# Four experts of a float32 mixture: column tiles of one width put one after another over four feature blocks

## The chip, the core and the metric

The kernel runs on one core of a Trainium2 chip. The metric is the device time of one execution in microseconds (us), as the median of several runs. One further execution is recorded by the hardware profiler; all rows shown below are from that one.

## The reference

A trunk of two layers over 256 positions of width 1024, all in float32. What matters here is the last sub-layer, a mixture of eight experts of which each position takes two:

```
logits = h @ w_router
top_v, top_i = lax.top_k(logits, TOP_K)          # TOP_K = 2 of N_EXPERTS = 8
gates = jax.nn.softmax(top_v, axis=-1)
...
for e in range(N_EXPERTS):
    y = y + dense_gate[..., e:e + 1] * swiglu(h, w_gate[e], w_up[e], w_down[e])

def swiglu(h, w_gate, w_up, w_down):
    return (jax.nn.silu(h @ w_gate) * (h @ w_up)) @ w_down
```

An expert's gate and up matrices are 1024 x 3584, its down matrix 3584 x 1024.

## The kernel before, in words

The experts are sorted by how many positions chose them; the rank in that order decides how many places an expert gets. Rank 0 has 128 places. Ranks 1 to 3 (`SMALL`) have 64 (`PLACES`). Ranks 4 to 7 (`MIDDLE`) have 64 and 32 more (`MORE`), 96 in all. They run in the order `RANKS`: 0, 1, 7, 6, 2, 5, 4, 3. Positions beyond the places go through a branch at the end (`overflow`).

**Weights.** An expert's weights come in 84 halves of 512 KB (128 x 1024 float32); eight experts have 672. `Stream` loads them in a fixed order into the pool `wp` of 30 tiles (`NW`), all through SP's queue (line 159). Each load takes the tile that was loaded 30 loads earlier and waits until the last reader of that tile is done; eight loads are on the way at most. When the program is written, `Stream` counts the tiles in use (`live`) and writes loads ahead while `live` is below `NW - ROOM`. `ROOM` is 4 in all of the expert part.

**Steps.** An expert of ranks 1 to 7 has 3584 hidden features in seven groups of 512. They are done in four steps: three long ones of two groups side by side, and a short one of the last group, split into two of 256 columns. A step computes gate (`pg`) and up (`pu`), then the product `act`, then `act` is transposed (`psT`). One step later comes its share of the output (`y`). For the short step that share is done by `down_half`, one output half at a time, and it falls behind the first `both` or `up_gate` of the next expert.

**Tiles of TensorE.** 64 places fill half the columns of the 128 x 128 array, so two such matmuls, with other weights, run side by side (`halves_of`). For the middle ranks the 32 further places go into four 32-wide column tiles side by side: `pm` holds up and gate of both groups, `ym` the output. `both` goes through the eight 128-row blocks of the 1024 features one by one: for each, gate and up with 64-wide tiles (line 1205), then the four 32-wide ones (line 1207). `down` and `down_half` do the same for `y` (lines 1263 and 1285) and `ym` (line 1233). A float32 matmul stands in the trace as two records, a pass each.

**Small work between.** `st.soon(n, ...)` puts a piece of work off by n beats, and a beat is one half drawn from the stream (`next(ws)`). In this way the gather of the next expert's positions (`psg`, read by ScalarE into `hs`), the transposes (`psT`, `psTm`) and the scatter of the last expert's output (`pssc`, read by VectorE) get their places among the matmuls. Gather, transposes and scatter share two PSUM buffers (`pst`). The engines run their instructions in the order in which the program has them.

Of the kernel before, what the change touches and what calls it, by code (L numbers as in the profile page):

```python
# [23 lines left out]
KD = D // P  # L24
S = 256
# [9 lines left out]
RANKS = (0, 1, 7, 6, 2, 5, 4, 3)  # L35
SMALL = (1, 2, 3)
PLACES = 64
MIDDLE = (4, 5, 6, 7)
MORE = 32
# [14 lines left out]
def trunk_(es, tc, stream, experts, blocks, x, xT, c, columns, ada_w, ln_g, ln_b, ev_w_in, pool_w, ev_sink, ev_w_out,  # L54
          od_w_in, od_sg_ln_g, od_sg_ln_b, w_sT, od_b_s, od_w_out, ffn_w_gate, ffn_w_up, ffn_w_down, out):
    nc = tc.nc
    V, A, G, T = nc.vector, nc.scalar, nc.gpsimd, nc.tensor
# [201 lines left out]
    st = Stream()  # L259
# [189 lines left out]
    with ExitStack() as ph:  # L449
# [50 lines left out]
        for g, w in enumerate(WINDOWS):  # L500
            r = w // 2
# [44 lines left out]
        h = big([P, KD, S], F32, name="h")  # L546
# [153 lines left out]
        for g in range(4):  # L700
            psg.append(bank())
            for t in range(NT):
                T.matmul(psg[g][:, 0:S], lhsT=pt[:, t, g * P:(g + 1) * P], rhs=band[:, g, t, :],
                         start=t == 0, stop=t == NT - 1)
# [5 lines left out]
        for g in range(4):  # L710
            ps = psg[g][:, S:2 * S]
# [4 lines left out]
        ws = []  # L716
# [91 lines left out]
        ws = [list(st.get()) for _ in range(2)]  # L808
# [14 lines left out]
        z, h = norm_modulate(y, gates[0, 2], folded, hf, gu_tile)  # L823
# [77 lines left out]
        ws = list(st.get()) + list(st.get())  # L901
# [6 lines left out]
        z, h = norm_modulate(y, gates[0, 5], (sa, sb), hf, v_half)  # L908
# [15 lines left out]
        for n in range(2):  # L924
            if n:
                ps2 = [psa.tile([P, 512], F32, tag="a", name="psv") for _ in range(NT)]
                for u in range(2):
                    for k, w in enumerate(st.get()):
                        kk = u * 4 + k
# [5 lines left out]
        for t in range(NT):  # L935
            mv = sml.tile([P, 2], F32, tag="mv", name="mv")
            V.bn_aggr(mv, s6s[t])
            mu, rs = rstd_of(mv)
# [4 lines left out]
        for u in range(4):  # L943
            if u == 3:
                st.AHEAD = 4
            ps = psa.tile([P, 2, S], F32, tag="a", name="psu")
# [7 lines left out]
        for g in range(0, 8, 2):  # L954
            ps = psa.tile([P, 2, NT, P], F32, tag="a", name="pssv")
# [114 lines left out]
    with ExitStack() as ph:  # L1070
# [118 lines left out]
        def both(step, h, pg, pu, pm):  # L1189


            s, fs = step
            ws = st.get()
            for kk in range(0, KD, 2):
                w = [next(ws) for _ in range(4 * len(fs))]
                for k in range(2):
                    if len(fs) == 2:
                        g, u = (w[k], w[2 + k]), (w[4 + k], w[6 + k])
                    else:
                        g, u = ((a[:, 0:S], a[:, S:2 * S]) for a in (w[k], w[2 + k]))  # L1200
                    n = g[0].shape[-1]
                    flags = dict(start=kk + k == 0, stop=kk + k == KD - 1)
                    for ps, pair in ((pg, g), (pu, u)):
                        for rows_, a in zip(halves_of, pair):
                            T.matmul(ps[rows_, 0:n], lhsT=h[:, kk + k, 0:PLACES], rhs=a, **flags)  # L1205
                    for b, a in enumerate(u + g):
                        T.matmul(pm[b * MORE:(b + 1) * MORE, 0:n], lhsT=h[:, kk + k, PLACES:], rhs=a, **flags)  # L1207
            for _ in ws:
                pass

# [40 lines left out]
        def down(step, aT, y):  # L1251
            s, fs = step
            small = RANKS[s] in SMALL + MIDDLE
            if fs[-1] == NFE - 1:
                for n in range(2):
                    down_half(step, aT, y, n)
            elif small:
                ws = st.get()
                for kk in range(4):
                    pair = [next(ws) for _ in range(2)]  # L1260
                    for n in range(2):
                        for rows_, w in zip(halves_of, pair):
                            T.matmul(y[n][rows_, :], lhsT=aT[0][:, kk, rows_], rhs=w[:, n * 512:(n + 1) * 512],  # L1263
                                     start=fs[0] == 0 and kk == 0, stop=False)
                    if RANKS[s] in MIDDLE:
                        for b, w in enumerate(pair):
                            down_more(aT[1], kk, b, [(n, w[:, n * 512:(n + 1) * 512]) for n in range(2)], y[2],
                                      fs[0] == 0 and kk == 0, False)
                for _ in ws:
                    pass  # L1270
            else:
                for u in range(2):
                    for k, w in enumerate(st.get()):
                        kk = u * 2 + k
                        for n in range(2):
                            mm3(y[n], sl2(aT, lambda a: a[:, kk, :]), sl2(w, lambda a: a[:, n * 512:(n + 1) * 512]),
                                fs[0] == 0 and kk == 0, False)

        def down_half(step, aT, y, n):

            ws = list(st.get())
            if RANKS[step[0]] in SMALL + MIDDLE:
                for k in range(2):
                    for b, rows_ in enumerate(halves_of):
                        T.matmul(y[n][rows_, :], lhsT=aT[0][:, k, rows_], rhs=ws[b * 2 + k], start=False, stop=k == 1)  # L1285
                    if RANKS[step[0]] in MIDDLE:
                        for b in range(2):
                            down_more(aT[1], k, b, [(n, ws[b * 2 + k])], y[2], False, k == 1)
            else:
                for k, w in enumerate(ws):  # L1290
                    mm3(y[n], sl2(aT, lambda a: a[:, k, :]), w, False, k == 3)
# [159 lines left out]
        for i, step in enumerate(steps):  # L1451
# [17 lines left out]
            if (s, fs[0]) == (1, 2):  # L1469
                for t in range(NT):  # L1470
                    A.activation(xt[t], xt[t], AF.Copy, scale=ALPHA)
            if (s, fs[0]) == (3, 0):
                lng, lnb = affine_rows(1, 1)
            h, ohT = cur
# [150 lines left out]
```

## Time and profile before

| | |
|---|---|
| median of 3 runs | 1353.6 us (1352.05 to 1355.18) |
| profiled execution | 1348.47 us, span 1346.7 us |
| TensorE matmul (PE) busy | 1315.8 us, 98% of the span |
| VectorE (DVE) busy | 522.9 us, 39% |
| ScalarE (ACT) busy | 323.1 us, 24% |
| DMA | 470.49 MB, mean 349 GB/s |
| granted TensorE clock, mean | 0.996 of full speed |

Busy is the time in which at least one instruction of the engine was running. Matmuls are pipelined and their ends are modelled, so starts say more of TensorE than durations do. The rank 7 expert starts at 619 us, rank 2 at 886.9, rank 5 at 976.1 and rank 3 at 1241 us; the last matmul of the experts ends about 1334 us.

### The profile page before, as it was taken

The page shows a single profiled execution, that of the slowest core. Times are in us where ns is not written, and L with a number is a line of the kernel's source. Part 1 is how long each engine was busy: PE and PEld are TensorE (multiplying, and loading weights), DVE is VectorE, ACT ScalarE, POOL GpSimd, SP SyncE. Part 2 cuts the span into 40 slices and gives each one's busy share as a digit, 9 for nine tenths or more (in the row PEclk, how much of TensorE's full clock was granted, in tenths as well). Part 3 has the DMA queues.
Part 4 walks back from the last instruction along what each step waited for, and adds up shares of the span by engine and source line. Part 5 has one row for each costly group of instructions (what it writes and reads, how often), then busy time and mean ns, then how long its engine had stood idle before and what let it go on. Part 6 is the DMA issues. An engine that isn't in the chain of part 4 may idle for free. (4 is left out here: it accounts for less than half of the span.)

```text
span 1346.7 us, 19701 instructions
## 1 busy us (share of the span) xinstructions
PE 1315.8 (98%) x7360; PEld 675.1 (50%) x7360; DVE 522.9 (39%) x812; ACT 323.1 (24%) x504; POOL 16.5 (1%) x82
## 2 busy tenths in 40 slices
PE   6999999999998999999999999999999999999997
PEld 4758999987866887442323233324423222323332
DVE  7697999947856986300200020012011001100102
ACT  0416444426227774310110011001001001100100
POOL 1000000000000000000000000000000000000001
PEclk9999999999989999999999999999999999999999
DMA  9997889991874799999999988999999998889993
GB/s 376 409 409 278 330 328 360 363 365 69 333 297 156 277 341 358 409 409 409 409 409 409 409 347 303 375 365 409 409 409 409 409 377 316 307 322 371 404 409 123
DMA packets 129576, 470.49 MB, mean 349 GB/s; under 512 B 14520, under 2 KB 14656, under 8 KB 129472
## 3 DMA queue, kind: packets, MB, share of 16 engines
q1 hardware_dynamic: 129168, 468.89, 90.0%
q8 instruction: 59, 0.97, 0.3%
q14 instruction: 45, 0.37, 0.1%
q10 hardware_dynamic: 304, 0.27, 0.1%
HBM read 468.05 MB, written 1.05 MB: 348 GB/s over the span
## 5 line engine op out<-in xcount | busy, mean ns | idle before, releaser
L196 DVE TENSOR_TENSOR lo<-raw,hi 128x1024 fp32r<-128x1024 f32 x158 | 186.4, 1220 | 32.1 <-ACT hi L195 25.6
L195 ACT ACTIVATE hi<-raw 128x1024 fp32r<-128x1024 f32 x158 | 159.0, 1053 | 67.0 <-PE y L371 12.8
L1263 PE MATMUL y<-raw,ah 128*64 128x512 f32 x672 | 160.4, 602 | 0.3 <-DMA raw<-in_experts 0.2
L1493 DVE TENSOR_TENSOR act<-act,pu 128x512 f32<-128x512 f32 (+1 forms) x16 | 9.9, 621 | 317.4 <-PE pu L1205 317.4
L1205 PE MATMUL pg<-raw,hs 128*64 128x512 f32 (+1 forms) x512 | 125.5, 564 | 0.2 <-DMA raw<-in_experts 0.2
L1207 PE MATMUL pm<-raw,hs 128*32 128x512 f32 (+1 forms) x1024 | 122.7, 551 | 0.0
L271 DVE CUSTOM_DVE_ANT_0 raw<-raw,cond,colt 128x1024 f32<-128x1024 f32 x96 | 118.7, 1281 | 8.2 <-DMA raw<-in_stream 8.2
L1205 PE MATMUL pu<-raw,hs 128*64 128x512 f32 (+1 forms) x512 | 119.0, 539 | 0.4 <-DMA raw<-in_experts 0.3
L1488 ACT ACTIVATE act<-pg 128x512 f32<-128x512 f32 (+1 forms) x35 | 19.4, 554 | 345.7 <-PE pg L1205 258.2
L369 PE MATMUL psgu<-hh,hi 128*128 128x256 f32 x320 | 91.2, 285 | 0.0
L371 PE MATMUL psgu<-hh,lo 128*128 128x256 f32 x320 | 90.6, 283 | 0.0
L370 PE MATMUL psgu<-hl,hi 128*128 128x256 f32 x320 | 89.9, 281 | 0.0
L1263 PEld LDWEIGHTS y<-raw,ah 128*64 128x64 f32 x672 | 43.5, 136 | 91.1 <-issue 76.2
L1185 PE MATMUL pu<-raw,hs 128*64 128x512 f32 (+1 forms) x384 | 76.6, 542 | 0.0
L1185 PE MATMUL pg<-raw,hs 128*64 128x512 f32 (+1 forms) x384 | 75.4, 541 | 0.0
L1498 DVE TENSOR_TENSOR act<-act,pu 128x512 f32<-128x512 f32 (+1 forms) x19 | 12.2, 643 | 147.3 <-PE pu L1185 147.3
L1205 PEld LDWEIGHTS pg<-raw,hs 128*64 128x64 f32 x512 | 25.6, 134 | 84.9 <-issue 76.5
L1233 PE MATMUL ym<-raw,am 128*32 128x512 f32 x448 | 68.0, 605 | 0.0
L1205 PEld LDWEIGHTS pu<-raw,hs 128*64 128x64 f32 x512 | 36.9, 137 | 61.1 <-issue 52.8
L1207 PEld LDWEIGHTS pm<-raw,hs 128*32 128x32 f32 x1024 | 20.1, 108 | 90.2 <-issue 87.0
L1333 DVE SCALAR_TENSOR_TENSOR x<-pssc,by_rank,x 128x512 f32<-128x512 f32 x28 | 20.8, 748 | 104.6 <-PE pssc L1331 104.6
L369 PEld LDWEIGHTS psgu<-hh,hi 128*128 128x128 f32 x320 | 60.7, 190 | 0.4
(303 smaller groups left out, 1655.4 us busy)
## 6 DMA issues: line engine op xcount, KB each, us to landing
raw<-in_experts SPq DMA_DIRECT2D x668, 512.0 KB, 10.1
raw<-in_stream SPq DMA_DIRECT2D x204, 512.0 KB, 7.4
lng<-in_ln_g SPq DMA_DIRECT2D x4, 512.0 KB, 7.9
lnb<-in_ln_b SPq DMA_DIRECT2D x4, 512.0 KB, 9.0
xT<-in_xT SPq DMA_DIRECT2D x2, 512.0 KB, 7.7
x<-in_x SPq DMA_DIRECT2D x2, 512.0 KB, 10.2
guest<-in_experts SPq DMA_DIRECT2D x2, 512.0 KB, 10.1
guests<-in_experts SPq DMA_DIRECT2D x2, 512.0 KB, 6.8
```

The costliest lines, as they stand in the source:

```text
L195: A.activation(hi, raw, AF.Copy)
L196: V.tensor_tensor(lo, raw, hi, op=ALU.subtract)
L271: V.tensor_tensor_reduce(raw[:, 0, :], raw[:, 0, :], cond, 1.0, adab[:, i:i + 1], ALU.mult, ALU.add, accum_out=mod[l, part][:, kk:kk + 1])
L369: T.matmul(ps, lhsT=l[0], rhs=r[0], start=start, stop=False)
L370: T.matmul(ps, lhsT=l[0], rhs=r[1], start=False, stop=False)
L371: T.matmul(ps, lhsT=l[1], rhs=r[0], start=False, stop=stop)
L1185: T.matmul(ps[rows_, 0:w.shape[-1]], lhsT=h[:, kk + k, :], rhs=w, start=kk + k == 0, stop=kk + k == KD - 1)
L1205: T.matmul(ps[rows_, 0:n], lhsT=h[:, kk + k, 0:PLACES], rhs=a, **flags)
L1207: T.matmul(pm[b * MORE:(b + 1) * MORE, 0:n], lhsT=h[:, kk + k, PLACES:], rhs=a, **flags)
L1233: T.matmul(y[q * MORE:(q + 1) * MORE, :], lhsT=am[:, k, b * MORE:(b + 1) * MORE], rhs=a, start=first, stop=last)
L1263: T.matmul(y[n][rows_, :], lhsT=aT[0][:, kk, rows_], rhs=w[:, n * 512:(n + 1) * 512], start=fs[0] == 0 and kk == 0, stop=False)
L1333: V.scalar_tensor_tensor(yacc[t][:, sl], ps, gate_by[:, t, r:r + 1], yacc[t][:, sl], op0=ALU.mult, op1=ALU.add)
```

## The change

For the middle ranks the feature blocks are taken four at a time: all gate matmuls of the four, then all up matmuls, then all 32-wide ones. In `down` all four blocks of `y` come ahead of all four of `ym`, and in `down_half` both blocks of `y` ahead of both of `ym`. The halves for a group are drawn from the stream before its matmuls are written. `ROOM` becomes 9 for middle ranks and stays 4 for the others. No matmul, load or other operation is added or left out.

```diff
--- before.py
+++ after.py
@@ -1191,20 +1191,25 @@
 
             s, fs = step
             ws = st.get()
-            for kk in range(0, KD, 2):
-                w = [next(ws) for _ in range(4 * len(fs))]
-                for k in range(2):
-                    if len(fs) == 2:
-                        g, u = (w[k], w[2 + k]), (w[4 + k], w[6 + k])
-                    else:
-                        g, u = ((a[:, 0:S], a[:, S:2 * S]) for a in (w[k], w[2 + k]))
-                    n = g[0].shape[-1]
-                    flags = dict(start=kk + k == 0, stop=kk + k == KD - 1)
-                    for ps, pair in ((pg, g), (pu, u)):
-                        for rows_, a in zip(halves_of, pair):
-                            T.matmul(ps[rows_, 0:n], lhsT=h[:, kk + k, 0:PLACES], rhs=a, **flags)
+
+            for k0 in range(0, KD, 4):
+                rs = []
+                for u in range(2):
+                    w = [next(ws) for _ in range(4 * len(fs))]
+                    for k in range(2):
+                        if len(fs) == 2:
+                            rs.append((k0 + u * 2 + k, (w[k], w[2 + k]), (w[4 + k], w[6 + k])))
+                        else:
+                            rs.append((k0 + u * 2 + k, *((a[:, 0:S], a[:, S:2 * S]) for a in (w[k], w[2 + k]))))
+                n = rs[0][1][0].shape[-1]
+                flags = lambda kk: dict(start=kk == 0, stop=kk == KD - 1)
+                for i, ps in ((1, pg), (2, pu)):
+                    for r in rs:
+                        for rows_, a in zip(halves_of, r[i]):
+                            T.matmul(ps[rows_, 0:n], lhsT=h[:, r[0], 0:PLACES], rhs=a, **flags(r[0]))
+                for kk, g, u in rs:
                     for b, a in enumerate(u + g):
-                        T.matmul(pm[b * MORE:(b + 1) * MORE, 0:n], lhsT=h[:, kk + k, PLACES:], rhs=a, **flags)
+                        T.matmul(pm[b * MORE:(b + 1) * MORE, 0:n], lhsT=h[:, kk, PLACES:], rhs=a, **flags(kk))
             for _ in ws:
                 pass
 
@@ -1256,13 +1261,16 @@
                     down_half(step, aT, y, n)
             elif small:
                 ws = st.get()
+                pairs = []
                 for kk in range(4):
                     pair = [next(ws) for _ in range(2)]
+                    pairs.append(pair)
                     for n in range(2):
                         for rows_, w in zip(halves_of, pair):
                             T.matmul(y[n][rows_, :], lhsT=aT[0][:, kk, rows_], rhs=w[:, n * 512:(n + 1) * 512],
                                      start=fs[0] == 0 and kk == 0, stop=False)
-                    if RANKS[s] in MIDDLE:
+                if RANKS[s] in MIDDLE:
+                    for kk, pair in enumerate(pairs):
                         for b, w in enumerate(pair):
                             down_more(aT[1], kk, b, [(n, w[:, n * 512:(n + 1) * 512]) for n in range(2)], y[2],
                                       fs[0] == 0 and kk == 0, False)
@@ -1283,7 +1291,8 @@
                 for k in range(2):
                     for b, rows_ in enumerate(halves_of):
                         T.matmul(y[n][rows_, :], lhsT=aT[0][:, k, rows_], rhs=ws[b * 2 + k], start=False, stop=k == 1)
-                    if RANKS[step[0]] in MIDDLE:
+                if RANKS[step[0]] in MIDDLE:
+                    for k in range(2):
                         for b in range(2):
                             down_more(aT[1], k, b, [(n, ws[b * 2 + k])], y[2], False, k == 1)
             else:
@@ -1469,6 +1478,8 @@
             if (s, fs[0]) == (1, 2):
                 for t in range(NT):
                     A.activation(xt[t], xt[t], AF.Copy, scale=ALPHA)
+            if fs[0] == 0 and s > 0:
+                st.ROOM = 9 if RANKS[s] in MIDDLE else 4
             if (s, fs[0]) == (3, 0):
                 lng, lnb = affine_rows(1, 1)
             h, ohT = cur
```

The order shows the effect on TensorE at two places. An entry names the line, the tile written, what is read, and the tile's columns by the moving columns; x8 stands for eight such matmuls, and a float32 matmul counts once here. The line numbers behind the change are those of the changed file.

First place: the second step of rank 7 in `both`, where the scatter of rank 1 (`pssc`) and the gather for rank 6 (`psg`) fall. Before:

```order
L1205 MATMUL pg<-raw,hs 64x512 x2
L1205 MATMUL pu<-raw,hs 64x512 x2
L1207 MATMUL pm<-raw,hs 32x512 x4
L1331 MATMUL pssc<-yhl,ohT 128x512 x2
L1088 MATMUL psg<-oh,z 128x96 x8
...
L1331 MATMUL pssc<-yhl,ohT 128x512 x4
```

And with the change:

```order
L1209 MATMUL pg<-raw,hs 64x512 x8
L1209 MATMUL pu<-raw,hs 64x512 x8
L1212 MATMUL pm<-raw,hs 32x512 x16
L1340 MATMUL pssc<-yhl,ohT 128x512 x2
L1088 MATMUL psg<-oh,z 128x96 x8
L1340 MATMUL pssc<-yhl,ohT 128x512 x4
```

The turn of 2, 2 and 4 matmuls, eight to a step, has become one of 8, 8 and 16, two to a step. Between the gather and the two further scatters (x4) there were two turns; now there is nothing.

Second place: `down` of the first step of rank 7, which follows. Before:

```order
L1263 MATMUL y<-raw,ah 64x512 x4
L1233 MATMUL ym<-raw,am 32x512 x4
...
L1219 MATMUL psT<-ident,act 128x128 x4
L1088 MATMUL psg<-oh,z 128x96 x8
L1224 MATMUL psTm<-ident,actm 128x64 x4
```

And with the change:

```order
L1270 MATMUL y<-raw,ah 64x512 x8
L1224 MATMUL psT<-ident,act 128x128 x4
L1088 MATMUL psg<-oh,z 128x96 x8
L1229 MATMUL psTm<-ident,actm 128x64 x4
L1270 MATMUL y<-raw,ah 64x512 x8
L1238 MATMUL ym<-raw,am 32x512 x16
```

The transposes and the second gather stood behind two blocks of `y` and `ym`; now they stand behind two blocks of `y`, in the middle of the 64-wide run. On SP's queue the loads keep their order; only the two row loads `lng` and `lnb` come five places earlier.

## Rows read from the trace of the kernel before

**Rows 1.** The page, its first line.
```profile
span 1346.7 us, 19701 instructions
```

**Rows 2.** Windows of four expert stretches: busy us and instructions by engine, granted clock, DMA.
```profile
619.00:886.90 267.90, 267.24 (x1608) 76.52 (x1606) 26.57 (x50) 22.81 (x49) 0.00 (x0) 1.00 0.97 379
886.90:976.10 89.20, 89.20 (x456) 34.21 (x454) 10.71 (x20) 9.93 (x22) 0.00 (x0) 1.00 1.03 408
976.10:1241.00 264.90, 264.90 (x1608) 76.23 (x1604) 26.97 (x52) 22.82 (x49) 0.00 (x0) 1.00 0.95 365
1241.00:1326.50 85.50, 84.81 (x418) 30.01 (x414) 9.46 (x14) 6.02 (x11) 0.00 (x0) 1.00 0.95 376
```

**Rows 3.** Waits of PE, 619 to 1326.5 us: us in total, times, longest.
```profile
PE pu L1205 <- DMA raw<-in_experts: 0.3, 1, 0.3
```

**Rows 4.** Timeline, rank 2 gate, weight loads alone: start, duration, engine, line.
```profile
888.28 0.14 PEld L1185 LDWEIGHTS pg<-raw,hs 128*64 128x64 f32 x2 [0.28 <-issue]
...
892.57 0.14 PEld L1185 LDWEIGHTS pg<-raw,hs 128*64 128x64 f32 x2 [0.29 <-issue]
```

**Rows 5.** Timeline, rank 7, `both` of a long step, TensorE alone.
```profile
702.90 1.08 PE L1205 MATMUL pg<-raw,hs 128*64 128x512 f32 x4
...
704.77 1.06 PE L1207 MATMUL pm<-raw,hs 128*32 128x512 f32 x8
705.76 1.08 PE L1205 MATMUL pg<-raw,hs 128*64 128x512 f32 x4
```

**Rows 6.** Timeline, rank 6, `down` of a long step, TensorE alone.
```profile
849.76 1.94 PE L1263 MATMUL y<-raw,ah 128*64 128x512 f32 x8
...
852.62 0.65 PE L1263 MATMUL y<-raw,ah 128*64 128x512 f32 x2
```

**Rows 7.** Timeline, 256-column steps: ranks 1 (pure) and 6 (mixed), TensorE alone.
```profile
603.16 3.62 PE L1185 MATMUL pg<-raw,hs 128*64 128x256 f32 x32
606.61 3.62 PE L1185 MATMUL pu<-raw,hs 128*64 128x256 f32 x32
...
862.19 0.65 PE L1205 MATMUL pg<-raw,hs 128*64 128x256 f32 x4
...
863.77 0.65 PE L1205 MATMUL pg<-raw,hs 128*64 128x256 f32 x4
```

**Rows 8.** Timeline, start of rank 7, TensorE alone.
```profile
618.95 0.64 PE L1205 MATMUL pg<-raw,hs 128*64 128x512 f32 x1
...
620.24 1.07 PE L1205 MATMUL pg<-raw,hs 128*64 128x512 f32 x2 [0.22 <-DMA raw<-in_experts]
...
633.39 1.08 PE L1205 MATMUL pg<-raw,hs 128*64 128x512 f32 x4
```

**Rows 9.** Timeline, rank 7, scatter and gather, TensorE and ScalarE.
```profile
661.01 0.73 PE L1331 MATMUL pssc<-yhl,ohT 128*128 128x512 f32 x2
...
661.58 1.92 PE L1088 MATMUL psg<-oh,z 128*128 128x96 f32 x16
...
663.43 1.08 PE L1205 MATMUL pg<-raw,hs 128*64 128x512 f32 x4
663.53 1.40 ACT L1096 ACTIVATE hs<-psg,f1sb,f1sa 128x96 f32<-128x96 f32 x4 [12.87 <-PE psg L1088]
```

**Rows 10.** DMA issues from 886.9 and from 976.1 us to the end.
```profile
raw<-in_experts SPq DMA_DIRECT2D x312, 512.0 KB, 10.1
...
raw<-in_experts SPq DMA_DIRECT2D x239, 512.0 KB, 9.7
```

**Rows 11.** Timeline, the end of the last expert: DMA issues and TensorE.
```profile
1300.77 11.82 SPq L159 DMA_DIRECT2D raw<-in_experts  x10
...
1319.32 7.09 PE L1263 MATMUL y<-raw,ah 128*64 128x512 f32 x32
```

**Rows 12.** The 32-wide weight loads: one group, and all of the line.
```profile
704.77 0.16 PEld L1207 LDWEIGHTS pm<-raw,hs 128*32 128x32 f32 x8 [0.81 <-issue]
...
L1207 PEld LDWEIGHTS pm<-raw,hs x1024: 106/108/109, 623.8 to 1228.4; 128*32 128x32 f32 x171
```

## The prediction

> **What bounds the kernel now.** The times are read first: the profiled execution took 1348.5 us, of which its span is 1346.7 [rows 1]; the three timed runs have a median of 1353.6, 5.1 us above it. A change of 0.2% (2.7 us) is about what a measurement of this kernel can tell from none. The sum below is made in microseconds of the profiled execution and taken off the median.
>
> The windows by expert come next [rows 2]. In all four stretches after the third expert begins TensorE is busy throughout, at a granted clock of 1.00 (the upper of its levels, 2.4 GHz), while VectorE and ScalarE are busy for about a tenth of the time. The waits say the same: the longest that a TensorE instruction spent on a DMA from 619 to 1326 us is 0.3 us [rows 3]. So the stretch is TensorE's, and what its own stream costs is the time. But the DMA column shows how near the second bound is: 408 GB/s in the stretch of rank 2, and 365 to 379 in the pairs of ranks 7, 6 and 5, 4. The weights come just in time, and this is the rival to watch.
>
> Then the timeline. A matmul here has two records (two passes). In a long run of 64-wide tiles of one kind, successive pairs of weight loads stand at 888.28 and 892.57, ten passes apart: 0.429 us for a pass of 512 columns on both halves of the array [rows 4]. Four 32-wide tiles side by side should take the same. In `both` a turn of one feature block is gate (2 passes), up (2) and the 32-wide rest (2): six passes, 2.574 us. The turn takes 705.76 - 702.90 = 2.86 us [rows 5]. In `down` it is 852.62 - 849.76 = 2.86 for the same six passes [rows 6]. In the short step (256 columns) a pass is (606.61 - 603.16)/16 = 0.216, six are 1.294, and the turn takes 863.77 - 862.19 = 1.58 [rows 7]. The excess is 0.286 to 0.289 us a turn. A turn has two changes of tile width, 64 to 32 and back, so a change costs about 0.144 us.
>
> **The change, part by part.** *Changes of width removed.* `both` goes from 8 turns a step to 2, in 16 steps: 96 turns fewer. `down` of a long step goes from 4 to 1, in 12 steps: 36 fewer. `down_half` goes from 2 to 1, twice for each of 4 experts: 8 fewer. That is 140 turns, or 280 changes. Against this, transposes and gathers that stood behind a 32-wide group now cut a 64-wide run in `down` (the second place shown in the order). Counted over the whole order of TensorE, from the first 32-wide matmul on, changes between widths 128, 64 and 32 fall from 444 to 172: 272 fewer (64 to 32: 192 to 52; 32 to 64: 160 to 36; to and from 128: 92 to 84). At 0.144 this is **39.2 us**. The few to and from 128 I price alike; they move the sum by little.
>
> Bounds of this price. Gate and up take 704.77 - 702.90 = 1.87 us, 0.154 over their four passes; the 32-wide group takes 705.76 - 704.77 = 0.99, 0.132 over two [rows 5]. No row of before has a run of 32-wide passes longer than two. If the 0.132 belongs to 32-wide work and not to the change back, a turn saves 0.154 alone: 140 x 0.154 = 21.6 us. If nothing is lost anywhere, it is 39.2. I take the upper, since the 64-wide side has the same excess, and there the long run shows that it isn't the work's own.
>
> The Trainium skill has a rule for this: TensorEngine Tiling (Array Packing), Key Properties, says that a change of tiling mode drains TensorE, and TensorE: Matmul & The Clock Gate, Part 2 (step by step, phases on the wall clock), puts a pipe drain at about 128 cycles. By the pages a change would cost an estimated 53 ns at 2.4 GHz, and the sum would be 272 x 0.053 = 14.5 us; the rows show almost three times that for one change, and the measurement decides.
>
> *Weights needed in another order.* For one 4-block group TensorE reads the gate halves of all four blocks before the first up half. Where the buffer is empty this costs. It is empty at one place, the start of rank 7: there the halves land one by one, 620.24 - 618.95 = 1.29 us apart, and four blocks are done at 633.39 [rows 8]. Taking 1.29 for each, the sixth half (the last that the gate needs) lands at 618.95 + 5 x 1.29 = 625.4. From there: two blocks of gate, 1.72; four of up, 3.43; a change; the 32-wide part, 3.43; a change: 634.3. The three turns saved in that group (0.86) don't arrive, and 0.9 more is lost: **-1.8 us**. At the start of rank 5, the next tightest, I allow another **-0.9**, see below.
>
> *Work emitted in one batch.* The queued small work is handed out while weights are fetched. Eight halves are now fetched ahead of a group in the long steps, where it was four. So a gather `psg` and two more scatters `pssc` stand together behind the first (the first place in the order). They share two PSUM buffers, so the last scatter waits until ScalarE has read the gather. Now: a scatter takes 661.58 - 661.01 = 0.57 us, the gather runs from 661.58 to 663.43, and ScalarE reads it in four `hs` from 663.53 for 1.40 us [rows 9], so until 664.9. After the change the second scatter would stand behind the gather, to 664.0, and the third would wait about 1.0 us. For ranks 6 and 4 a scatter has four matmuls in place of two, which covers some 0.5 of it. Two experts at 1.0 and two at 0.5: **-3.0 us**; between nothing, if the buffers come free sooner, and twice that.
>
> *ROOM = 9.* It changes when a load is written into the program, not what a load waits for: on SP's queue nothing moves but the two row loads `lng` and `lnb`, five places ahead. A load waits for the last reader of the tile 30 loads earlier, as before. Priced at nothing; the full ring of 30 tiles is its cover, and the buffer rival below is what it costs without it.
>
> *Buffers freed later.* The last reader of a half is its 32-wide matmul, now at the end of a group. Halves in all: 84 an expert, 672. Issued by the start of rank 2: 672 - 312 = 360; of rank 5: 672 - 239 = 433 [rows 10]. Consumed by then: 332 and 416 (four of the expert before come later). So rank 2 starts 28 ahead, near the 30 of the tile ring, and rank 5 starts 17 ahead, of which 8 are still on the way (10.1 us to land; 512 KB at the 408 GB/s of rank 2 are 1.28 us): 9 in hand. With the change the last `down` of rank 6 frees its eight halves within 3.5 us, in which the DMA brings three; about 5 fewer are ahead at rank 2, and 4 in hand at rank 5. That covers the gate of the first group but for a half or two; hence the 0.9 above. Do the pairs still refill the ring? Ranks 7 and 6 take 267.9 us now [rows 2], some 253 then; at 1.28 the DMA can issue 197, from 172 to 369, and the ring's ceiling is 362. For 5 and 4: 264.9 becomes some 248, 193 halves from 428, 621 against 614. Both refill, barely. At the end, ten loads are issued from 1300.77 on; the first of the last twelve, two earlier, lands near 1308.5, and TensorE takes it at 1319.32 [rows 11]: 11 us in hand, of which five halves take 6.4.
>
> The sum: 39.2 - 1.8 - 0.9 - 3.0 = 33.5 us. Profiled 1348.5 - 33.5 = 1315.0; median 1353.6 - 33.5 = **1320.1 us**.
>
> **The rivals.** *The ring is too shallow* (weights bound). For: the pairs refill it with some 7 halves to spare. If it fell to 21 tiles (the bookkeeping limit under ROOM 9 taken as real), rank 2 would begin 7 + 5 = 12 behind its old lead; 9 are in hand, and each missing half costs 1.28 us, once at rank 5 and once at the end: 3 x 1.28 x 2 = 7.7 us, so 1328. Against: 28 ahead at rank 2 is already above the 26 that the bookkeeping had (ROOM 4), so the hardware goes by the ring. Chance 12%.
>
> *The excess of the 32-wide group is its own.* Gain 21.6 - 5.7 = 15.9: 1338. Chance 7%.
>
> *The loads of 32-wide weights can't be hidden in a long run.* This is the one that ends slower. A load takes 108 ns, and all eight of a group stand within 0.16 us [rows 12]; if each pass had to wait for its four loads together, 384 such passes at 0.108 cost 41.5 us: 1320.1 + 41.5 = 1362. It decides from 33.5/384 = 0.087 us a pass. Against it: the 64-wide loads, in a run as long, add nothing to the 0.429 [rows 4]. The Trainium skill, TensorE: Matmul & The Clock Gate, Part 3 (What overlaps), states that a weight load overlaps running matmuls only when the row group differs; all tiles here use all 128 rows, so by it this rival would hold. The trace disagrees for the 64-wide tiles and has no row for the 32-wide. Chance 4%.
>
> *The change does nothing,* since the excess comes from something other than the change of width: 1353. The order shows the groups merged, and both turns show the excess with different operands. Chance 1%.
>
> **How the numbers follow.** The forecast holds 76%, with a range of its own of 1314 (no loss at all) to 1326 (losses twice as large). The range that holds 8 in 10 takes in most of the ring's case: 1313 to 1333. Faster: 0.76 + 0.12 + 0.07 = 0.95; within 0.2%: 0.01; slower: 0.04.
>
> **What would show it.** In the profile after: 16 records of `pg` and 16 of `pu` in a row, then 32 of `pm` in about 3.5 us; a change at 0.14; the long `both` near 21.2 us a step (22.9 now); one wait of about a microsecond in front of the third `pssc`; DMA waits at ranks 7 and 5 only; more GB/s in the pairs. It is wrong if `pm` runs take over 3.7 us, or if TensorE waits for DMA in rank 2 or the last expert.

## The result, and the profile after

| | before | with the change |
|---|---|---|
| median | 1352.8 us (1348.99 to 1355.18, 4 runs) | 1320.4 us (1318.97 to 1323.79, 4 runs) |
| ratio | | 0.9767, 95% interval 0.9735 to 0.9798 |
| span of the profiled execution | 1346.7 us | 1317.4 us |
| first gate matmul of rank 7 to last output matmul of the experts | 714.4 us | 682.1 us |

The change makes the kernel 32.4 us faster by the medians; 33.5 were forecast, as 1320.1 us. That the two medians meet to 0.3 us is in part luck, as the four runs of the kernel after range over 4.8 us. The last line of the table is the better measure: the code ahead of rank 7 is the same in both, but in the two profiled executions rank 7 starts at 618.9 and at 622.0 us. Most of that is the granted clock much earlier. From 356.2 to 363.0 us TensorE is busy throughout in both executions, as it is just before; the clock is 1.00 of full speed in the kernel before and 0.50 (the lower level, 1.2 GHz) in the kernel after, where 23 matmuls fall into the window in place of 38. The window in both, the kernel before first:

```profile
356.20:363.00 6.80, 6.80 (x38) 5.51 (x37) 4.24 (x7) 2.32 (x4) 0.00 (x0) 1.00 1.02 414
```

```profile
356.20:363.00 6.80, 6.80 (x23) 5.49 (x23) 4.41 (x7) 2.16 (x4) 0.00 (x0) 0.50 1.02 416
```

The stretch from rank 7 on became 32.3 us shorter. It is read from the first and last starts of two lines; these are the ones of the kernel after, in the view of the tiles `pg` and `y`:

```profile
L1209 PE MATMUL pg<-raw,hs x512: 379/592/644, 622.0 to 1195.5; 128*64 128x512 f32 x128, 128*64 128x256 f32 x43
...
L1293 PE MATMUL y<-raw,ah x112: 592/592/643, 647.8 to 1304.1; 128*64 128x512 f32 x112
```

1304.1 - 622.0 = 682.1. All experiments below are compared over this stretch.

The windows of the same four expert stretches, of the kernel after (ranks 7 and 6; 2; 5 and 4; 3), answer to [rows 2]:

```profile
622.00:874.50 252.50, 248.93 (x1610) 88.82 (x1608) 26.66 (x50) 22.84 (x49) 0.00 (x0) 1.00 1.00 395
874.50:963.10 88.60, 88.60 (x456) 34.56 (x454) 10.71 (x20) 9.93 (x22) 0.00 (x0) 1.00 1.02 405
963.10:1210.80 247.70, 246.45 (x1608) 88.44 (x1604) 27.05 (x52) 22.84 (x49) 0.00 (x0) 1.00 0.99 390
1210.80:1295.60 84.80, 84.21 (x418) 30.35 (x414) 9.45 (x14) 6.02 (x11) 0.00 (x0) 1.00 1.02 403
```

The pairs take 252.5 and 247.7 us in place of 267.9 and 264.9. The last column is the other half of the story: 395 and 390 GB/s where there were 379 and 365, and 403 in the last expert where there were 376. The DMA's slack has nearly gone.

The timeline of the second group of four blocks in the first step of rank 7 after, TensorE alone, answers to [rows 5]; a line is now one tile over all four blocks:

```profile
637.25 3.65 PE L1209 MATMUL pg<-raw,hs 128*64 128x512 f32 x16
640.73 3.60 PE L1209 MATMUL pu<-raw,hs 128*64 128x512 f32 x16
644.26 3.64 PE L1212 MATMUL pm<-raw,hs 128*32 128x512 f32 x32
647.84 1.94 PE L1293 MATMUL y<-raw,ah 128*64 128x512 f32 x8
```

A turn of four blocks takes 647.84 - 637.25 = 10.59 us. Its 24 passes at the 0.429 of [rows 4] are 10.30, so two changes of width cost 0.29. The 32-wide run alone is 647.84 - 644.26 = 3.58, eight passes and 0.15. A long run of 32-wide passes goes at 0.429 like the 64-wide. The same for 256 columns and for `down`, rank 6 after, which answer to [rows 6, 7]:

```profile
852.17 1.95 PE L1209 MATMUL pg<-raw,hs 128*64 128x256 f32 x16
...
857.63 1.95 PE L1209 MATMUL pg<-raw,hs 128*64 128x256 f32 x16
```

```profile
865.61 5.37 PE L1270 MATMUL y<-raw,ah 128*64 128x512 f32 x24
870.91 3.64 PE L1238 MATMUL ym<-raw,am 128*32 128x512 f32 x32
874.48 1.94 PE L1185 MATMUL pg<-raw,hs 128*64 128x512 f32 x8
```

One turn of four short blocks is 857.63 - 852.17 = 5.46 (four old turns: 6.32); the 32-wide run of `down` is 874.48 - 870.91 = 3.57.

Where TensorE waited, by the waits of the kernel after from 600 to 1300 us (in all, times, longest):

```profile
PE pg L1209 <- DMA raw<-in_experts: 2.3, 3, 1.9
PE total L1560 <- PEq L1526: 1.8, 1, 1.8
PE pssc L1340 <- DVE x L1342: 1.7, 2, 0.8
PE pssc L1340 <- ACT hs L1096: 0.8, 2, 0.4
```

Three have grown or are new. The weights are late at the start of rank 7 (2.3 us; 0.5 before). The scatters wait, 2.5 us in all. And `total`, behind the branch at the end, waits 1.8 us where it waited 0.3. The last was not forecast.

### The profile page after: what moved, and what is told of

The parts are those of the page before. It is cut to its first block, busy times and chain, and to the rows that moved or that the text cites. A ratio compares the mean times of both kernels' runs of the same rounds, so it can differ in the third digit from the quotient of the medians.

```text
span 1317.4 us, 19701 instructions
## 1 busy us (share of the span) xinstructions
PE 1280.9 (97%) x7360; PEld 702.6 (53%) x7360; DVE 522.9 (40%) x812; ACT 323.2 (25%) x504; POOL 16.5 (1%) x82
## 5 line engine op out<-in xcount | busy, mean ns | idle before, releaser
L196 DVE TENSOR_TENSOR lo<-raw,hi 128x1024 fp32r<-128x1024 f32 x158 | 186.3, 1219 | 32.3 <-ACT hi L195 25.5
L1270 PE MATMUL y<-raw,ah 128*64 128x512 f32 x672 | 154.7, 598 | 0.2 <-DMA raw<-in_experts 0.2
L1209 PE MATMUL pg<-raw,hs 128*64 128x512 f32 (+1 forms) x512 | 105.6, 545 | 2.3 <-DMA raw<-in_experts 2.3
L1212 PE MATMUL pm<-raw,hs 128*32 128x512 f32 (+1 forms) x1024 | 102.8, 542 | 0.0
L1209 PE MATMUL pu<-raw,hs 128*64 128x512 f32 (+1 forms) x512 | 102.5, 539 | 0.0
L1185 PE MATMUL pu<-raw,hs 128*64 128x512 f32 (+1 forms) x384 | 76.6, 542 | 0.0
L1185 PE MATMUL pg<-raw,hs 128*64 128x512 f32 (+1 forms) x384 | 75.4, 542 | 0.0
L1209 PEld LDWEIGHTS pg<-raw,hs 128*64 128x64 f32 x512 | 34.3, 136 | 65.5 <-issue 53.4
L1212 PEld LDWEIGHTS pm<-raw,hs 128*32 128x32 f32 x1024 | 30.0, 109 | 69.8 <-issue 65.6
L370 PEld LDWEIGHTS psgu<-hl,hi 128*128 128x128 f32 x320 | 60.7, 190 | 0.4
L371 PEld LDWEIGHTS psgu<-hh,lo 128*128 128x128 f32 x320 | 60.3, 188 | 0.0
```

The lines of the kernel that those rows point to most:

```text
L196: V.tensor_tensor(lo, raw, hi, op=ALU.subtract)
L370: T.matmul(ps, lhsT=l[0], rhs=r[1], start=False, stop=False)
L371: T.matmul(ps, lhsT=l[1], rhs=r[0], start=False, stop=stop)
L1185: T.matmul(ps[rows_, 0:w.shape[-1]], lhsT=h[:, kk + k, :], rhs=w, start=kk + k == 0, stop=kk + k == KD - 1)
L1209: T.matmul(ps[rows_, 0:n], lhsT=h[:, r[0], 0:PLACES], rhs=a, **flags(r[0]))
L1212: T.matmul(pm[b * MORE:(b + 1) * MORE, 0:n], lhsT=h[:, kk, PLACES:], rhs=a, **flags(kk))
```

## The experiments

The theory is that each change of tile width (128, 64 or 32 columns) costs TensorE about 0.144 us, and the kernel after has 272 fewer of them. The rivals: the excess belongs to 32-wide work itself, to each going over to another PSUM tile, or the gain is that of `ROOM`. Each ratio is against the kernel before in the runs beside that kernel; the stretch is from the profiled execution.

| run | median us | ratio (95% interval) | stretch us | shorter by | width changes |
|---|---|---|---|---|---|
| before | 1352.8 | | 714.4 | | 444 |
| e1_both_alone | 1326.3 | 0.9825 (0.9786 to 0.9864) | 691.3 | 23.1 | 248 |
| e2_down_alone | 1344.8 | 0.9938 (0.9915 to 0.9961) | 704.8 | 9.6 | 368 |
| e3_room_alone | 1352.2 | 1.0007 (0.9988 to 1.0025) | 714.4 | 0.0 | 444 |
| e4_two_blocks | 1324.7 | 0.9790 (0.9754 to 0.9826) | 686.6 | 27.8 | 256 |
| e0_the_change | 1318.3 | 0.9764 (0.9735 to 0.9792) | 682.3 | 32.1 | 172 |
| e5_as_landed | 1321.4 | 0.9768 (0.9746 to 0.9790) | 681.0 | 33.4 | 172 |
| e6_scatter_apart | 1316.7 | 0.9741 (0.9718 to 0.9764) | 681.0 | 33.4 | 178 |
| e9_all_three | 1316.6 | 0.9737 (0.9715 to 0.9760) | 680.8 | 33.6 | 154 |
| e7_ring26 | 1337.1 | 0.9906 (0.9881 to 0.9932) | 693.1 | 21.3 | 172 |
| e12_ring26_before | 1355.8 | 1.0042 (1.0027 to 1.0057) | 715.4 | -1.0 | 444 |
| e10_order_and_scatter | 1319.3 | 0.9772 (0.9753 to 0.9790) | 678.2 | 36.2 | 178 |
| e11_turned_later | 1315.1 | 0.9734 (0.9708 to 0.9759) | 680.4 | 34.0 | 157 |

**e1_both_alone.** Of the diff, only the part in `both` and the `ROOM` lines.

```diff
@@ both
-            for kk in range(0, KD, 2):
+            for k0 in range(0, KD, 4):
...
@@ down, down_half: as before
```

> Only the gate and up part (both) takes four feature blocks at a time; the output part (down, down_half) stays as before. Width theory (each change between 64-, 32- and 128-wide matmuls costs TensorE 0.144 us): changes fall from 444 to 248, 196 x 0.144 = 28.2 us, less 1.7 for the weights that come late at the start of rank 7 and 2.5 for the scatters written in one batch: 24 us faster than before, some 8 slower than the full change. Rival, the excess belongs to 32-wide work: 96 turns x 0.154 = 14.8, less 4.2: about 11 us faster. Rival, the gain is ROOM's: as much as the full change, 32 us.

The stretch is 23.1 us shorter. Its waits are those of the full change to a tenth, but for the one at the end, which is the 0.3 of before. With the 1.8 that the late weights add and the 2.5 of the scatters put back, 196 changes gave 27.4 us: 0.140 each. The rival of 11 us is out.

**e2_down_alone.** The other half: `down` and `down_half` with the `ROOM` lines, `both` as before.

```diff
@@ down
-                    if RANKS[s] in MIDDLE:
-                        for b, w in enumerate(pair):
+                    pairs.append(pair)
...
+                if RANKS[s] in MIDDLE:
+                    for kk, pair in enumerate(pairs):
+                        for b, w in enumerate(pair):
```

> Only the output part (down, down_half) puts its 64-wide matmuls ahead of its 32-wide ones; gate and up stay as before. Width theory: changes fall from 444 to 368, 76 x 0.144 = 10.9 us faster, and neither the late weights at rank 7 nor the scatter batch arises, so nothing is taken off: 11 us. Rival, the excess belongs to 32-wide work: 44 turns x 0.154 = 6.8 us. Rival, the gain is ROOM's: 32 us.

9.6 us shorter, though the branch at the end cost 1.5 us here and 0.3 before. Put back, 10.8 us for 76 changes: 0.142 each. By the rival it would be 6.8.

**e3_room_alone.** The kernel before and two lines.

```diff
+            if fs[0] == 0 and s > 0:
+                st.ROOM = 9 if RANKS[s] in MIDDLE else 4
```

> The kernel before with the ROOM rule of the change alone (9 for ranks 4 to 7, 4 for the others); no matmul moves. Width theory: a load waits for the last reader of the tile 30 loads earlier whatever ROOM is, so no change, within 2 us of before. Rival, the earlier or later writing of the loads makes the weights come in better time: several us faster, up to the whole 32. Rival, ROOM 9 holds only 21 tiles in use: some 8 us slower, with waits of TensorE for weights at rank 5 and in the last expert.

The stretch is the same to a tenth of a microsecond, the ratio 1.0007. `ROOM` does nothing by itself; both rivals are out.

**e4_two_blocks.** Groups of two feature blocks.

```diff
-            for k0 in range(0, KD, 4):
+            for k0 in range(0, KD, 2):
                 rs = []
-                for u in range(2):
+                for u in range(1):
...
-                if RANKS[s] in MIDDLE:
-                    for kk, pair in enumerate(pairs):
+                    if RANKS[s] in MIDDLE and kk % 2:
+                        for j, pair in pairs:
```

> The change with groups of two feature blocks in place of four, in both and in down. Width theory: changes fall from 444 to 296 and not to 172: 148 x 0.144 = 21.3 us faster than before; the weights are needed in the order in which they land and four halves are drawn at a time as before, so no late weights and no scatter batch: about 21 us, some 11 slower than the full change. Rival, the 32-wide excess is its own: 96 turns x 0.154 = 14.8 us. Rival, what gains is the long run of four blocks itself, whatever the number of changes: little of the 32 us.

27.8 us shorter, more than the 21.3 expected. The expectation added up the order wrongly: the five kinds of change in it (96, 68, 18, 46, 28) make 256 and not 296. So 188 changes are gone, which at 0.144 is 27.1. No wait for weights over 0.2 us and none for a scatter is left. Half the grouping gives 86% of the gain, since it is free of what the rest costs.

**e0_the_change** was the changed kernel once more, beside the next three.

> The changed kernel once more, on the chip of the three others, as what they are compared with. 32 us faster than before, about 1320 us; from the first gate matmul of rank 7 to the last output matmul 682 us, with about 1.9 us of waiting for weights at the start of rank 7 and 2.5 us of waiting in front of scatters.

682.3 us, with the same waits to a tenth.

**e5_as_landed.** In each group TensorE goes over between the gate and the up tile twice more, and the number of width changes stays.

```diff
-                for i, ps in ((1, pg), (2, pu)):
-                    for r in rs:
-                        for rows_, a in zip(halves_of, r[i]):
+                for j in range(0, 4, 2):
+                    for i, ps in ((1, pg), (2, pu)):
+                        for r in rs[j:j + 2]:
+                            for rows_, a in zip(halves_of, r[i]):
...
```

> The change with the 64-wide matmuls of a group in the order in which the weights land: gate of two blocks, up of the same two, gate of the next two, up of these; then the 32-wide ones of all four. Widths change as often as in the change. Width theory: going between the gate and the up tile costs nothing; the wait for weights in the first group of rank 7 falls from 1.9 to about 0.5 us, so 1 to 2 us faster than the change. Rival, what costs is each going over to another PSUM tile, not to another width: two more of them in each of 32 groups, 64 x 0.144 = 9.2 us slower than the change.

681.0 us, 1.3 less than the change, where the rival had 9.2 more. Another PSUM tile of the same width costs nothing that shows. In the waits of e5 the one for weights has gone from 2.3 to 0.4 us:

```profile
PE pssc L1341 <- DVE x L1343: 1.7, 2, 0.8
...
PE pg L1210 <- DMA raw<-in_experts: 0.4, 2, 0.2
```

**e6_scatter_apart.** A scatter's addition and the next scatter's matmuls stand seven beats apart in place of one.

```diff
                     V.scalar_tensor_tensor(yacc[t][:, sl], ps, gate_by[:, t, r:r + 1], yacc[t][:, sl],
                                            op0=ALU.mult, op1=ALU.add)
-                    yield 1
+                    yield 7
```

> The change with seven beats in place of one between a scatter's addition and the next scatter's matmuls, so that one group of four blocks draws one scatter and not three. Theory: the waits of the third scatter (twice 0.84, twice 0.4 us, 2.5 in all) go; changes of width go from 172 to 178, 0.9 us: 1.6 us faster than the change. Rival, the wait only moves: another instruction waits for the same PSUM buffer, no difference or slower by 0.9 us.

681.0 us, 1.3 less. The two largest waits of TensorE from 600 us on:

```profile
PE total L1560 <- PEq L1526: 3.0, 1, 3.0
PE pg L1209 <- DMA raw<-in_experts: 2.3, 3, 1.9
```

The scatter waits are gone, as expected. But `total` waits 3.0 us where it waited 1.7 in e0, so that the end gives back half of what the middle won; without that it would be 2.6 less. That is 1.0 more than expected. The six changes that are added are all to or from 128 columns, and were priced at 0.9: what a change to or from 128 costs isn't shown by these runs, and here six of them cost little or nothing.

**e9_all_three.** Both, and the second group of a step turned round.

```diff
+                if k0:
+                    more()
                 for j in range(0, 4, 2):
...
+                if not k0:
+                    more()
```

Here `more()` writes the group's 32-wide matmuls.

> The change with both of these, and with the second group of four blocks in a step turned round: its 32-wide matmuls first, behind those of the first group. Width theory: changes fall from 172 to 154, 18 x 0.144 = 2.6 us, plus 1.4 for the weights in order and 2.5 for the scatters: about 6.5 us faster than the change, 1314 us. Rival, the 32-wide matmuls of the second group need all eight of its halves at once and give them back later, so weights come late at rank 7, rank 5 and in the last expert: no faster than the change, with TensorE waits for weights of several us in the profile.

680.8 us, 1.5 less than the change and not 6.5. The rival holds at rank 7, though not at rank 5, which takes 120.6 us where the change takes 121.4. The timeline at the start of rank 7 shows the turned group standing still:

```profile
630.79 5.36 PE L1209 MATMUL pm<-raw,hs 128*32 128x512 f32 x48
638.30 1.04 PE L1209 MATMUL pm<-raw,hs 128*32 128x512 f32 x2 [2.15 <-DMA raw<-in_experts]
```

The 32-wide matmuls of the second group need its last halves 2.2 us before they are there. In ranks 6 and 4 the turn saved: 125.1 us each, 126.3 in the change and 125.9 in e6. From e6 that is 0.9 for six changes between 64 and 32 fewer in each rank, the price once more. And `total` waited 3.0 us again.

**e7_ring26** and **e12_ring26_before.** One line, in the changed kernel and in the kernel before.

```diff
-    NW = 30
+    NW = 26
```

> The change with a ring of 26 weight tiles in place of 30. Read from the first gate matmul of rank 7 to the last output matmul (682 us with the change), since the earlier layers use the ring too. Theory: in the change rank 5 starts 13 halves ahead, 5 of them in hand, and the last twelve halves land about 5 us before they are needed; four tiles fewer take 5.1 us from both: 3 to 6 us longer, with waits for weights at the start of rank 5 or in the last expert. Rival, what is on the way (eight loads) is all that counts: no difference, no new wait. Rival, the middle ranks themselves run dry, since a group holds eight halves to its end: 20 us longer or more, with waits in ranks 6 and 4.

> The kernel before with a ring of 26 tiles in place of 30, read over the same stretch (714.4 us before). Theory: there rank 5 starts with 9 halves in hand and the last expert has 11 us; four tiles take 5.1 us from each: no more than 1 us longer, so the cut costs the kernel before less than the changed one. Rival, the cut costs both the same.

The kernel before takes 1.0 us longer over the stretch, the changed one 10.8: rank 5 takes 126.8 us in place of 121.4, the last expert 98.8 in place of 93.2, ranks 7, 6, 2 and 4 what they took. The places are those of the theory; the size, 3 to 6 us, was meant for both together and is what each of them took. All of rank 5's 5.4 us falls in its first group, which takes 15.95 us where e0 takes 10.54: with the buffer empty it goes like the first group of rank 7 (15.26 in the change). The 0.7 above that is not shown to be the ring's. Behind a wait of 1.91 us there, with TensorE busy for 1.37 of 3.40 us, the granted clock fell from 1.00 to 0.50 (1.2 GHz) for 3.4 us; the first group of rank 7 in the change has such a wait and no lower clock. The windows of e7:

```profile
971.00:974.40 3.40, 1.37 (x4) 0.39 (x6) 0.00 (x0) 0.00 (x0) 0.00 (x0) 1.00 1.03 410
974.40:977.80 3.40, 3.40 (x10) 0.98 (x8) 0.00 (x0) 0.00 (x0) 0.00 (x0) 0.50 1.02 408
```

The 1.0 of the kernel before is all at the branch, 1.3 us of `total` waiting in place of 0.3. Here are first the waits of the changed kernel with 26 tiles, then of the kernel before with 26:

```profile
PE pg L1209 <- DMA raw<-in_experts: 4.5, 5, 1.9
PE total L1560 <- PEq L1526: 3.5, 1, 3.5
...
PE y L1270 <- DMA raw<-in_experts: 1.6, 6, 0.5
PE pu L1185 <- DMA raw<-in_experts: 0.9, 4, 0.3
```

```profile
PE total L1549 <- PEq L1515: 1.3, 1, 1.3
PE pu L1185 <- DMA raw<-in_experts: 0.7, 3, 0.3
...
PE y L1263 <- DMA raw<-in_experts: 0.5, 2, 0.3
```

So the ring of 30 was near enough for the change, with fewer than four tiles to spare.

**e10_order_and_scatter** is e5 and e6 together.

> The change with the 64-wide matmuls in the order in which weights land, and with the scatters one to a group (the two parts that each took 1.2 us off the stretch from rank 7 to the last output matmul). Theory: they add up: 682.2 - 1.2 - 1.2 = 679.8 us, 2.4 faster than the change. Rival, one gives back what the other brings, by a wait for weights at rank 5 or in the last expert: 681 us.

678.2 us, 4.1 less than the change where 2.4 were expected. Without the branch e5 gave 1.2 and e6 2.6, and these add up; the branch's wait, which hid half of e6, is 1.3 us here where it is 1.7 in e0.

**e11_turned_later** is e10 with the turned group in all steps but the first of rank 7.

```diff
+                turned = k0 and (s, fs[0]) != (2, 0)
+                if turned:
+                    more()
...
+                if not turned:
+                    more()
```

> The same as the kernel with order and scatter, and the second group of a step turned round (32-wide first) in all steps but the first of rank 7. There the turned group waited 2.2 us for weights; in ranks 6 and 4 it saved 0.9 us each. Changes of width fall from 178 to 157 counted without it: 21 x 0.144 = 3.0 us. Theory: 679.8 - 3.0 = 676.8 us over the stretch, 5 faster than the change. Rival, the wait for weights comes up at the start of rank 5 in its place: 679 or more.

680.4 us where 676.8 were expected. Ranks 6 and 4 gave 0.8 and 0.9 us, as before. But the rival came true at the start of rank 5, by its timeline:

```profile
964.67 6.24 PE L1209 MATMUL pm<-raw,hs 128*32 128x512 f32 x50
971.15 1.92 PE L1209 MATMUL pm<-raw,hs 128*32 128x512 f32 x14 [0.23 <-DMA raw<-in_experts]
973.00 1.94 PE L1218 MATMUL pg<-raw,hs 128*64 128x512 f32 x8
```

Sixteen 32-wide passes in a row, two groups of them, take 973.00 - 964.67 = 8.33 us, where 16 x 0.429 = 6.86 and a change make 7.0: 1.3 us of waiting for weights. The rest was lost at the end. First the timeline of the last `y` ahead of the branch and the `total` behind it, then the windows around the stand:

```profile
1281.70 7.09 PE L1278 MATMUL y<-raw,ah 128*64 128x512 f32 x32
1291.67 5.37 PE L1568 MATMUL total<-x,ident 128*128 128x512 f32 x8 [2.88 <-PEq L1534]
```

```profile
1286.00:1288.50 2.50, 2.50 (x14) 0.72 (x10) 0.00 (x0) 0.00 (x0) 0.00 (x0) 1.00 0.96 382
1288.50:1291.60 3.10, 0.29 (x2) 0.00 (x0) 0.00 (x0) 0.00 (x0) 0.00 (x0) 1.00 0.25 82
1291.60:1295.00 3.40, 3.33 (x5) 1.56 (x6) 0.00 (x0) 0.00 (x0) 0.00 (x0) 0.58 0.03 10
```

TensorE, busy throughout until then, stood still for 2.9 us, and the granted clock was 0.58 of full speed in the 3.4 us after, which is mostly the lower of its levels, 1.2 GHz. The eight records of `total` took 5.4 us; in the other kernels they take 3.7 (in e10 they start at 1290.53, and the next matmul at 1294.13). That is 1.7 us more, and 1.6 more of waiting than in e10 makes 3.3: the last expert takes 96.1 us in place of 92.8. By the medians e11 has the lowest ratio, 0.9734, but its interval overlaps those of the change and of e6 and e9; none of them is shown to be faster than the change by its time. Over the stretch e10 is the shortest.

## Why the prediction was right, step by step

*The price of a change of width* held. It was taken at 0.144 us from one turn. The runs, with their new waits put back, give 27.4/196 = 0.140 (e1), 10.8/76 = 0.142 (e2), 27.8/188 = 0.148 (e4) and (32.3 + 1.8 + 2.5 + 1.5)/272 = 0.140 for the change. Four counts lie on one line, so the gain goes with the number of changes, not with the length of a run or with the place. Nearly all of these changes are between 64 and 32: those to and from 128 are eight fewer in e1 and in the change, and as many as before in e2 and e4. Counted without them the four are 0.146, 0.142, 0.148 and 0.144. That the prediction priced the few to and from 128 alike is not borne out, by these counts or by e6. The lower bound, an excess of the 32-wide work itself (21.6 us), fell by the 3.58 us of eight passes. Why one costs 0.14 is not shown. The Trainium skill (TensorEngine Tiling (Array Packing), Key Properties) says that a change of tiling mode drains TensorE, and the runs agree in so far as a change costs time. The estimate of 53 ns worked out from its pipe drain (TensorE: Matmul & The Clock Gate, Part 2) is far from the measured 140.

*The slower rival*, 32-wide loads that can't be hidden, fell with the same row. The Trainium skill (TensorE: Matmul & The Clock Gate, Part 3, What overlaps) would have them wait, since all tiles use the same rows. The trace disagrees: 32 records with as many loads went at the pace of the 64-wide.

*The weights late at rank 7* were priced at 1.8 us, 0.9 of it a turn saving that doesn't arrive. The timeline of the start after answers to [rows 8]:

```profile
621.99 0.64 PE L1209 MATMUL pg<-raw,hs 128*64 128x512 f32 x1
...
623.26 1.93 PE L1209 MATMUL pg<-raw,hs 128*64 128x512 f32 x6 [0.20 <-DMA raw<-in_experts]
627.11 1.07 PE L1209 MATMUL pg<-raw,hs 128*64 128x512 f32 x2 [1.91 <-DMA raw<-in_experts]
...
637.25 3.65 PE L1209 MATMUL pg<-raw,hs 128*64 128x512 f32 x16
```

The first group takes 637.25 - 621.99 = 15.26 us; before it took 14.44. It lost 0.82, against 0.9 in the sum. The wait of 1.91 is for the third block's gate, as foreseen, and e5 removes it. *At rank 5*, 0.9 was allowed and nothing came: no wait for weights stands there. The loads from the start of ranks 2 and 5 on, in the view of the DMA issues, answer to [rows 10]:

```profile
raw<-in_experts SPq DMA_DIRECT2D x314, 512.0 KB, 10.1
...
raw<-in_experts SPq DMA_DIRECT2D x243, 512.0 KB, 10.1
```

672 - 314 = 358 at rank 2 and 672 - 243 = 429 at rank 5: 26 and 13 ahead, two and four less than before, where five less was worked out. The rival of a ring cut to 21 tiles, 12 less at rank 2, is out with this.

*The scatters* were priced at 3.0 us and cost 2.5, twice 0.84 and twice 0.4. The timeline of the first of them answers to [rows 9]:

```profile
663.71 1.92 PE L1088 MATMUL psg<-oh,z 128*128 128x96 f32 x16
...
665.41 0.71 PE L1340 MATMUL pssc<-yhl,ohT 128*128 128x512 f32 x2
665.66 1.40 ACT L1096 ACTIVATE hs<-psg,f1sb,f1sa 128x96 f32<-128x96 f32 x4 [12.01 <-PE psg L1088]
666.16 0.75 DVE L1342 SCALAR_TENSOR_TENSOR x<-pssc,by_rank,x 128x512 f32<-128x512 f32 x1 [1.50 <-PE pssc L1340]
...
666.97 0.73 PE L1340 MATMUL pssc<-yhl,ohT 128*128 128x512 f32 x2 [0.84 <-DVE x L1342]
```

The third scatter starts at 666.97, by its row released by VectorE, whose read of the second scatter ends at 666.91. ScalarE's read of the gather ends only at 667.06, when the third scatter is already under way. So here, and at rank 5, it waited for VectorE, where the prediction had it wait for ScalarE; that 0.84 is near the predicted 1.0 is luck, since the two reads end 0.15 us apart. The 0.4 at ranks 6 and 4 is put down to ScalarE, as foreseen. e6 shows that both go when the scatters stand apart.

*The end* is the term that was missing. The prediction saw 11 us in hand at the last twelve halves, five halves lost, and no cost. But the profile after shows `total` waiting 1.8 us. The rows of the last loads and of the branch, kernel after:

```profile
1283.20 4.17 SPq L159 DMA_DIRECT2D raw<-in_experts  x4
...
1288.54 7.09 PE L1270 MATMUL y<-raw,ah 128*64 128x512 f32 x32
...
1297.43 2.81 PE L1560 MATMUL total<-x,ident 128*128 128x512 f32 x6 [1.80 <-PEq L1526]
```

What costs here is the branch itself. It stands on TensorE's queue with its length in ns and its start, in the view of its line, before and after:

```profile
L1515 PEldq COMPARE_BRANCH  x1: 3832/3832/3832, 1322.0 to 1322.0; - x1
```

```profile
L1526 PEldq COMPARE_BRANCH  x1: 4632/4632/4632, 1292.5 to 1292.5; - x1
```

Before, it starts 4.4 us ahead of the end of the last `y` in front of it (1326.41), takes 3.8 us and is over in time. After, it starts at 1292.48, only 3.15 us ahead of that end (1295.63), takes 4.63 and is over at 1297.11; `total` follows 0.29 us later. The wait is 4.63 + 0.29 - 3.15 = 1.77 us. The traces of all kernels agree. Where the wait is 0.3 us (before, e1, e3, e4), the branch starts 4.4 us ahead and takes 3.8 to 3.9. In the other ten it starts 1.9 to 4.1 us ahead, takes 4.3 to 5.2, and `total` follows its end by 0.29 us.

The weights set its start. In these ten kernels the branch starts 0.05 or 0.06 us after the landing of the last half that this `y` reads (after: 1292.42); in the four others that half had landed 2.1 to 4.7 us before the branch (4.3 in before, so that the five halves lost, 6.4 us, were more than was in hand here). The last load of all is issued 14 us ahead of the end of that `y` in before and 8.6 us ahead in after, so the same halves land later against TensorE's work. Why a branch takes 3.8 to 5.2 us on TensorE, where on the queues of the other engines it takes 0.05 to 0.07, and why it is longer in the ten, is not shown.

*The sum.* 39.2 - 1.8 - 2.5 - 1.5 = 33.4, and 32.3 were measured; the terms that were off (rank 5 by 0.9 and the scatters by 0.5 too dear, the end by 1.5 too cheap) nearly cancel. The 1.1 left over is 0.004 on each of the 272 changes, or just what the eight to and from 128 among them were priced at.

## What to carry to other kernels

Count the changes of tile width in TensorE's order, and price one from a turn against a long run of one width; group the work by width, but only as far as the buffers hold the weights longer and the weights come in the order in which they are then read. Grouping by two already gave most of the gain, without a new wait. After such a gain, look for the next bound where the slack was: against the 408 GB/s of [rows 2] the DMA had 7 and 11% free in the pairs before, and 3 and 4% after, and a ring four tiles smaller, which cost the kernel before 1.0 us, cost the changed one 10.8.

## What the runs showed that was not expected

- A branch at the end, around work that isn't needed here, takes TensorE's queue 3.8 to 5.2 us. It makes TensorE stand for 0.3 to 3.5 us, longer where the last weights in front of it land so late that it starts late.
- One such stand of 2.9 us was followed by a granted clock of 0.58 over 3.4 us, where it had been 1.00 (e11), which cost 1.7 us more; stands of 3.0 us in e6 and e9 and of 3.5 in e7 were not (`total` took 3.7 us there). A stand of about this length was followed by a lower clock in one run and not in three.
- Going from one PSUM tile to another of the same width costs TensorE nothing that can be measured (e5), while going from 64 to 32 columns and back costs 0.14 us each way on average.
